# Feed-forward layers of an encoder on one core: four low parts made by ScalarE and adding transfers in place of VectorE, and one bank's copy put ahead of a high part

## The chip, the cores and the metric

The kernel runs on one core of one Trainium2 chip. The metric is the device time of one execution in microseconds, as a median of several runs. The profile that is read here is of one execution and has its own time.

## What is computed

The program is the trunk of a bidirectional encoder: two interleaved layers (attention, then a gated short convolution as token mixer), each followed by a squared-ReLU feed-forward layer and a gated embedding. The two request groups have 512 and 256 tokens and share the weights; the kernel runs them as 768 columns. The change is in the feed-forward part, the line with `mlp_w_up`:

```python
for i in range(DEPTH):                      # 2 layers
    h = rms_norm(x, norm_mix[i])
    x = x + (window_attention if i % 2 == 0 else short_conv)(h, ...)
    h = rms_norm(x, norm_mlp[i])
    x = x + jnp.square(jax.nn.relu(h @ mlp_w_up[i])) @ mlp_w_down[i]   # 1024 -> 4096 -> 1024
    gate = jax.nn.sigmoid(rms_norm(x, norm_ple[i]) @ ple_w_gate[i])
    x = x + (p[i] @ ple_w_proj[i]) * gate
return rms_norm(x, final_norm)
```

All of it is float32. The kernel splits each operand of a matmul into a high part in the matmul's own rounded type (fp32r) and a low part, the remainder, and adds three products: high by high, high by low, low by high.

## The kernel before

**The seven products.** In the feed-forward layers a product of two by two blocks is done with seven products instead of eight (Strassen's scheme), so weights and activations are also needed in sums. For the weights of one job (`Weights7`, two fetched tiles of 128x1024, `wraw`) these are: `direct` (keys w11, w12), `w22`, `s32` (the sum of which s3 and s2 are the halves) and `s14` (s1, s4). `sums32` and `sums14` form the sums on VectorE (L479, L480, L484, L485) in the tiles `sum0` and `sum1`. Each group then needs a high part (a copy on ScalarE, L504, into `whi`, `zhi` or `vhi`) and a low part (`wlo`, `zlo`, `vlo`). `s32` goes to the `z` tiles, of which there is one pair; `w22` to the `v` tiles, also one pair.

**Two ways to make a low part.** `low` (L532 for weights, L424 for activations) is one VectorE subtraction: source minus high part. `added` and `sum_added` do it without VectorE: ScalarE writes the negated high part into the low tile (L515, L524, L429), and then a DMA issued by GpSimd (POOL in the profile) adds the source onto it as it lands (L517 from DRAM for `w22`, L525 from the tile `sum0`, L430 from an activation tile). Before the change `w22` is done the second way in all these jobs, `s32` only once in a layer (in the last up job).

**Jobs.** A layer has 16 up jobs (each 256 of the 4096 hidden columns) and 16 down jobs, each of seven products. A product is 12 matmuls of 128x384. The order is written out by hand, `up` and `down` name the instructions of ScalarE, VectorE and TensorE in the order in which these engines run them, and each job prepares the weights of the next (`v = make()`). After the first two ups come seven groups of four jobs: an up, two downs, an up. So each group runs as first down, second down, **odd up**, and then the **even up** of the next group; the even up follows directly on an odd up and stands directly before a **first down**. Ups run their products in the order w11, s3, s2, w12, s1, w22, s4, into the banks a, b, a, c, a, d, a; so do downs, with two banks for each letter. Before s2 may write into bank a, ScalarE must have copied a to c (L1370; in downs L1454): that is "the first bank's copy". After s3 ScalarE copies b to p (L1377), after s2 it copies a to d (L1382).

**Activations of an up.** An up job leaves two tiles y1, y2. Their squares, four sums (t1, t3 in y1's tile; t4, t2 in y2's: L408 to L414) and their high and low parts are made by a list of eight steps (`acts_of`), which the next up works off between its own instructions (`late`): square y1; high part of x11; high part of x21 and x22 with their low parts and t1, t3; t4 and t2; high part of t1 and t3 (L418); high part of t4 and t2; low part of t1 and t3 (L424); low part of t4 and t2 (L424). The odd up works off the list of the even up before it, the even up that of the odd up before it, in both cases for the down jobs that come next; the first down begins right after the even up has worked off its list, and its product s2 reads, in its first four matmuls, the high and low part of t2 of one up and then of the other.

**What GpSimd does.** In these layers POOL issues only the adding transfers, in program order. SP issues the fetches of `wraw` (L111), of which three tiles exist.

## Time and profile before

| | |
|---|---|
| median of 3 runs | 1596.95 us (1595.84 to 1600.51) |
| the profiled execution | 1596.31 us, of which its span is 1594.5 us |
| mean granted TensorE clock | 0.995 |
| one group of four jobs (28 products) | 56.18 us, seven times a layer |
| TensorE idle (span less busy) | 48.5 us |
| VectorE and ScalarE busy from 490 to 900 us | 372.5 and 253.9 of 410 us |
| adding transfers issued by POOL | 72 (62 of L517, 6 of the gate weights L1643, 2 each of L430 and L525) |

The page gives, for each engine, its busy time; "PE" is TensorE's matmuls and "PEld" its weight loads. The recorded duration of a matmul (326 ns) is its way through the array; the next begins about 163 ns after it, so twelve take 1.95 us. In the timeline a row is a run of equal instructions with its start and length in us; in brackets stands how long the engine had been idle, and what ended that.

### The profile page before, as it was taken

The page shows a single profiled execution, that of the slowest core. Times are in us where ns is not written, and L with a number is a line of the kernel's source. Part 1 is how long each engine was busy: PE and PEld are TensorE (multiplying, and loading weights), DVE is VectorE, ACT ScalarE, POOL GpSimd, SP SyncE. Part 2 cuts the span into 40 slices and gives each one's busy share as a digit, 9 for nine tenths or more (in the row PEclk, how much of TensorE's full clock was granted, in tenths as well). Part 3 has the DMA queues.
Part 4 walks back from the last instruction along what each step waited for, and adds up shares of the span by engine and source line. Part 5 has one row for each costly group of instructions (what it writes and reads, how often), then busy time and mean ns, then how long its engine had stood idle before and what let it go on. Part 6 is the DMA issues. An engine that isn't in the chain of part 4 may idle for free.

```text
span 1594.5 us, 24379 instructions
## 1 busy us (share of the span) xinstructions
PE 1546.0 (97%) x9375; PEld 1485.2 (93%) x9375; DVE 1404.2 (88%) x2300; ACT 977.4 (61%) x1566; POOL 82.5 (5%) x116
## 2 busy tenths in 40 slices
PE   9999999999999999999989999999999999999996
PEld 7988889999999999999989999999999999999985
DVE  8599898899999899999898887869999999999997
ACT  7478766866566556657764344556656656655764
POOL 0211000010000000001000000000000000000000
PEclk9999999999999999999999999999999999999998
DMA  8854413443333333335512212122333333333432
GB/s 278 214 138 131 138 45 99 120 108 82 96 100 100 100 94 78 94 100 143 154 60 80 79 67 84 63 78 68 99 100 99 96 90 81 98 100 99 113 102 103
DMA packets 57461, 166.35 MB, mean 104 GB/s; under 512 B 7249, under 2 KB 10833, under 8 KB 57345
## 3 DMA queue, kind: packets, MB, share of 16 engines
q1 hardware_dynamic: 45440, 139.89, 27.2%
q0 software_dynamic: 11904, 24.91, 8.9%
q8 instruction: 73, 1.20, 0.3%
q14 instruction: 44, 0.35, 0.1%
HBM read 143.02 MB, written 10.48 MB: 96 GB/s over the span
## 4 chain that ended last, share of the span: by engine, by line
PE 46%; DVE 38%; ACT 10%; issue 4%; DMA 1%; SPq 0%; DVEq 0%; ACTq 0%
PE a L180 17%; PE mm L180 8%; PE B L180 4%; DVE t L424 4%; PE b L180 4%; PE C L180 4%; DVE wlo L532 4%; DVE y L1146 3%; DVE zlo L532 3%; PE gate L180 2%; DVE act L463 2%; PE c L180 2%; ACT y L1149 1%; DVE sum L480 1%; DVE sum L479 1%
## 5 line engine op out<-in xcount | busy, mean ns | idle before, releaser
L180 PE MATMUL a<-xs,whi 128*128 128x384 f32 x624 | 115.6, 328 | 3.0 <-DVE y L1393 1.6
L180 PE MATMUL a<-t,zhi 128*128 128x384 f32 x568 | 111.2, 329 | 2.9 <-ACT c L1370 2.9
L180 PE MATMUL a<-t,whi 128*128 128x384 f32 x568 | 109.4, 326 | 0.0
L180 PEld LDWEIGHTS a<-xs,whi 128*128 128x128 f32 x624 | 102.5, 189 | 5.8 <-DVE low L2047 2.5
L180 PE MATMUL b<-t,zhi 128*128 128x384 f32 x552 | 106.8, 326 | 0.3 <-DVE t L424 0.3
L504 ACT ACTIVATE vhi<-wraw 128x512 fp32r<-128x512 f32 x71 | 44.6, 628 | 98.9 <-PE B L180 81.3
L180 PE MATMUL a<-act,whi 128*128 128x384 f32 x512 | 104.1, 326 | 0.0
L1459 DVE TENSOR_TENSOR x<-x,a 128x384 f32<-128x384 f32 x128 | 70.3, 555 | 37.2 <-PE a L180 37.2
L180 PEld LDWEIGHTS a<-t,zhi 128*128 128x128 f32 x568 | 93.7, 189 | 7.7 <-ACT c L1370 6.4
L532 DVE TENSOR_TENSOR wlo<-wraw,whi 128x1024 fp32r<-128x1024 f32 x74 | 90.3, 1220 | 10.9 <-ACT whi L504 10.9
L1149 ACT ACTIVATE y<-y 128x768 f32<-128x768 f32 x62 | 51.9, 837 | 71.6 <-DVE y L1146 71.5
L180 PEld LDWEIGHTS a<-t,whi 128*128 128x128 f32 x568 | 94.9, 189 | 0.6 <-ACT d L1561 0.6
L532 DVE TENSOR_TENSOR wlo<-sum,whi 128x1024 fp32r<-128x1024 f32 x71 | 86.8, 1222 | 8.8 <-ACT whi L504 8.8
L180 PEld LDWEIGHTS b<-t,zhi 128*128 128x128 f32 x552 | 92.3, 189 | 0.9 <-DVE t L424 0.9
L504 ACT ACTIVATE whi<-sum 128x1024 fp32r<-128x1024 f32 x71 | 74.5, 1049 | 21.2 <-PE a L180 18.4
L180 PEld LDWEIGHTS a<-act,whi 128*128 128x128 f32 x512 | 86.6, 189 | 0.0
L504 ACT ACTIVATE zhi<-sum 128x1024 fp32r<-128x1024 f32 x71 | 74.9, 1054 | 19.1 <-DVE sum L480 19.1
L418 ACT ACTIVATE t<-y 128x768 fp32r<-128x768 f32 x64 | 53.8, 840 | 51.9 <-DVE y L409 45.5
L532 DVE TENSOR_TENSOR zlo<-sum,zhi 128x1024 fp32r<-128x1024 f32 x69 | 84.0, 1218 | 0.0
L504 ACT ACTIVATE whi<-wraw 128x1024 fp32r<-128x1024 f32 x76 | 79.7, 1048 | 3.7
L180 PE MATMUL mm<-xs_mix,whi 128*128 128x512 f32 (+1 forms) x320 | 77.3, 331 | 0.2 <-DVE pjs L610 0.2
L180 PE MATMUL b<-t,zlo 128*128 128x384 f32 x276 | 63.1, 332 | 10.7 <-DVE zlo L532 10.7
(335 smaller groups left out, 4389.6 us busy)
## 6 DMA issues: line engine op xcount, KB each, us to landing
wraw<-in_up SPq DMA_DIRECT2D x64, 512.0 KB, 4.2
wraw<-in_down SPq DMA_DIRECT2D x64, 512.0 KB, 4.4
wraw<-in_w_in SPq DMA_DIRECT2D x24, 512.0 KB, 3.4
vlo<-in_down POOLq DMA_DIRECT2D x32, 256.0 KB, 6.0
wraw<-in_gate SPq DMA_DIRECT2D x16, 512.0 KB, 3.8
vlo<-in_up POOLq DMA_DIRECT2D x28, 256.0 KB, 5.8
pj<-pjs SPq DMA_DIRECT2D x16, 384.0 KB, 2.9
wraw<-in_w_q SPq DMA_DIRECT2D x8, 512.0 KB, 4.7
```

Source lines behind the costliest of these rows:

```text
L180: pe.matmul(ps, lhsT=w, rhs=rhs, **flags)
L418: act.activation(t[0][:], (self.q1, self.q2)[i][:], AF.Copy)
L424: dve.tensor_tensor(lo[:], (self.q1, self.q2)[i][:], hi[:].bitcast(F32), ALU.subtract)
L463: dve.tensor_tensor(lo[:], self.q2[:], hi[:].bitcast(F32), ALU.subtract)
L479: dve.tensor_tensor(a[:, :512], r1[:, :512], r2[:, :512], ALU.add)
L480: dve.tensor_tensor(a[:, 512:], a[:, :512], r2[:, 512:], ALU.add)
L504: act.activation(hi[:], src, AF.Copy)
L532: dve.tensor_tensor(lo[:], src, hi[:].bitcast(F32), ALU.subtract)
L1146: dve.scalar_tensor_tensor(t[:, o:e], src, 0.0, r[:, o:e], op, ALU.mult)
L1149: act.activation(t[:], t[:], AF.Square)
L1459: dve.tensor_tensor(t[:, o : o + H], t[:, o : o + H], f, op)
```

## The change

It has four parts. In `acts_of` the last step, the low part of t4 and t2, is `added(1)` in place of `low(1)`: a negated copy on ScalarE and an adding transfer of 384 KB. In `up`, in `down` and in the first of the last two downs (`down_first`) the high part of `s32` is followed at once by `sum_added`'s negated copy and an adding transfer of 512 KB, and the subtraction on VectorE (`w.low("s32")` in the next job) finds nothing left to do. In `up` one step of the list that stood between product w11 and the first bank's copy now stands behind the copy. And `rest` in `down_first` loses its `low("s32")`.

```diff
@@ acts_of
                 lambda: e.high(0),
                 lambda: e.high(1),
                 lambda: e.low(0),
-                lambda: e.low(1),
+                lambda: e.added(1),
@@ up
             product7(a, w, "w11", xs, True)
-            if not first:
-                late()
             c = bank("A" if first else "C", "c")[:, :H]
             act.activation(c, a, AF.Copy)
-            late(5 if first else 1)
+            late(5 if first else 2)
@@ up
             if seven:
                 v.sums14()
-                (v.sum_added if final else lambda: v.high("s32"))()
+                v.sum_added()
@@ down, and the same line in down_first
             v.sums14()
-            v.high("s32")
+            v.sum_added()
@@ down_first
             def rest():
                 added(top, H, a, ALU.add)
-                v.low("s32")
                 v.low("s14")
                 less(p)
```

The two functions that it now calls more often stand as they were:

```python
def added(self, i):                       # Sums, activations
    hi, lo = self.t[i]
    act.activation(lo[:], hi[:].bitcast(F32), AF.Copy, scale=-1.0)
    nc.gpsimd.dma_start(lo[:], (self.q1, self.q2)[i][:], accum_op=ALU.add)

def sum_added(self):                      # Weights7
    self.high("s32")
    self.due.remove("s32")
    hi, lo, src = self.parts["s32"]
    act.activation(lo[:], hi[:].bitcast(F32), AF.Copy, scale=-1.0)
    nc.gpsimd.dma_start(lo[:], src, accum_op=ALU.add)
```

ScalarE's queue in an even up of the first layer, before (y and t are the activation tiles, t_5339 and t_5342 the high parts of t1, t3 and of t4, t2):

```order
L504 ACTIVATE whi<-sum 128x1024
L1149 ACTIVATE y_5232<-y_5232 128x768
L450 ACTIVATE act<-y_5232 128x384
L1370 ACTIVATE c<-a 128x384
L454 ACTIVATE act<-y_5233 128x768
L1377 ACTIVATE p<-b 128x384
L1382 ACTIVATE d<-a 128x384
L418 ACTIVATE t_5339<-y_5232 128x768
L418 ACTIVATE t_5342<-y_5233 128x768
L504 ACTIVATE zhi<-sum 128x1024
L504 ACTIVATE whi<-wraw 128x1024
L504 ACTIVATE vhi<-wraw 128x512
```

The same stretch of ScalarE's queue in the changed kernel, from the first bank's copy on:

```order
L1368 ACTIVATE c<-a 128x384
L450 ACTIVATE act<-y_5246 128x384
L454 ACTIVATE act<-y_5247 128x768
L1375 ACTIVATE p<-b 128x384
L1380 ACTIVATE d<-a 128x384
L418 ACTIVATE t_5352<-y_5246 128x768
L418 ACTIVATE t_5355<-y_5247 128x768
L504 ACTIVATE zhi<-sum 128x1024
L524 ACTIVATE zlo<-zhi 128x1024
L504 ACTIVATE whi<-wraw 128x1024
L429 ACTIVATE t_5356<-t_5355 128x768
L504 ACTIVATE vhi<-wraw 128x512
```

The copy of a to c has moved ahead of the high part of x11 (L450), and two negated copies, L524 and L429, stand around the high part of `direct`.

POOL's queue before, over two groups of four jobs, is these rows (each is the transfer of `w22`, one for a job):

```order
L517 DMA vlo<-in_down 128x512 x2
L517 DMA vlo<-in_up 128x512 x2
L517 DMA vlo<-in_down 128x512 x2
L517 DMA vlo<-in_up 128x512 x2
L517 DMA vlo<-in_down 128x512 x2
```

POOL's queue in the changed kernel, from an odd up over the even up and the two downs to the next odd up (t_5207 and t_5356 are the low parts of t4, t2):

```order
L525 DMA zlo<-sum 128x1024
L430 DMA t_5207<-y_4822 128x768
L517 DMA vlo<-in_up 128x512
L525 DMA zlo<-sum 128x1024
L430 DMA t_5356<-y_5247 128x768
L517 DMA vlo<-in_down 128x512
L525 DMA zlo<-sum 128x1024
L517 DMA vlo<-in_down 128x512
L525 DMA zlo<-sum 128x1024
L517 DMA vlo<-in_up 128x512
```

A group of four jobs had four transfers in POOL's queue and has ten; in an up job they are three, in the order zlo, t, vlo. In the whole program VectorE's queue loses 86 instructions (56 of L532 into zlo, 30 of L424), and ScalarE and POOL gain 86 each.

## The prediction
> **What bounds the kernel now.** First the page's busy times, then TensorE's waits:

> ```profile
> PE 1546.0 (97%) x9375; PEld 1485.2 (93%) x9375; DVE 1404.2 (88%) x2300; ACT 977.4 (61%) x1566; POOL 82.5 (5%) x116
> ...
> PE b L180 <- DVE zlo L532: 10.7, 17, 0.7
> PE c L180 <- ACT xs L372: 4.6, 1, 4.6
> PE a L180 <- ACT c L1370: 2.9, 12, 0.2
> ```

> TensorE sets the end; what VectorE saves is worth only TensorE's waits. Two kinds recur in the feed-forward layers, and the change aims at both: on `zlo`, and on the first bank's copy c. The waits show too little, since a matmul's row (326 ns) covers half of a gap. The chain of waits in order of time gives a group's true cost:

> ```profile
> 459.74 1.98 PE a L180 x12
> 461.72 1.95 PE C L180 x12
> ...
> 515.92 1.98 PE a L180 x12
> ```

> A group takes 515.92 - 459.74 = 56.18 us; its 28 products of 1.95 us are 54.6. So **1.58 us are lost in a group**, 22 us in the 14. The timeline of an even up and the first down behind it shows where:

> ```profile
> 499.90 0.81 PE L180 MATMUL b<-t,zlo 128*128 128x384 f32 x4
> 500.00 0.52 ACT L450 ACTIVATE act<-y 128x384 fp32r<-128x384 f32 x1
> 500.43 0.47 ACT L1370 ACTIVATE c<-a 128x384 f32<-128x384 f32 x1
> 500.96 1.57 PE L180 MATMUL a<-t,zhi 128*128 128x384 f32 x8 [0.24 <-ACT c L1370]
> ...
> 512.83 0.81 PE L180 MATMUL b<-t,zhi 128*128 128x384 f32 x4
> 513.08 1.22 DVE L532 TENSOR_TENSOR zlo<-sum,zhi 128x1024 fp32r<-128x1024 f32 x1
> 514.35 0.59 PE L180 MATMUL b<-t,zlo 128*128 128x384 f32 x2 [0.71 <-DVE zlo L532]
> ```

> Four matmuls after 499.90 (0.65 us), s2 could begin at 500.55; it begins at 500.96 with its next matmul 0.1 late too: 0.5 lost. Four after 512.83 `zlo` is wanted at 513.48 and comes at 514.35: 1.0 lost.

> **The change, part by part.** Prices of one instruction:

> ```profile
> L532 DVE TENSOR_TENSOR zlo<-sum,zhi x69: 1214/1218/1225, 325.3 to 1498.9; 128x1024 fp32r<-128x1024 f32 x69
> L424 DVE TENSOR_TENSOR t<-y,t 128x768 fp32r<-128x768 f32 x64 | 60.8, 952 | 0.1
> L524 ACT ACTIVATE zlo<-zhi x2: 1057/1057/1057, 716.8 to 1477.3; 128x1024 fp32r<-128x1024 f32 x2
> L429 ACT ACTIVATE t<-t x2: 824/832/839, 317.7 to 321.0; 128x768 fp32r<-128x768 f32 x2
> ```

> VectorE loses 56 x 1.22 + 30 x 0.95 = 97 us, ScalarE gains 56 x 1.06 + 30 x 0.83 = 84 us. Neither is a term of the sum: ScalarE, at 61%, has room on average. What counts is when POOL's transfers land, and here a second set of rows decides:

> ```profile
> 319.48 0.88 POOL L430 DMA_DIRECT2D t<-q  x1 [5.75 <-ACT t L418]
> 321.00 0.84 ACT L429 ACTIVATE t<-t 128x768 fp32r<-128x768 f32 x1
> 323.62 0.89 POOL L430 DMA_DIRECT2D t<-q  x1 [3.26 <-ACT whi L504]
> 325.54 0.64 ACT L515 ACTIVATE vlo<-vhi 128x512 fp32r<-128x512 f32 x1
> 327.75 0.88 POOL L517 DMA_DIRECT2D vlo<-in_up  x1 [3.24 <-ACT t L418]
> ...
> 718.27 0.87 POOL L525 DMA_DIRECT2D zlo<-sum  x1 [10.02 <-ACT zlo L524]
> 721.22 0.63 ACT L515 ACTIVATE vlo<-vhi 128x512 fp32r<-128x512 f32 x1
> 723.27 0.90 POOL L517 DMA_DIRECT2D vlo<-in_down  x1 [4.12 <-issue]
> ...
> t<-q POOLq DMA_DIRECT2D x2, 384.0 KB, 3.8
> zlo<-sum POOLq DMA_DIRECT2D x2, 512.0 KB, 4.7
> ```

> Read each transfer against the ScalarE copy that it needs. The copy for the transfer of 323.62 ended at 321.84, that for 327.75 at 326.18, that for 723.27 at 721.85: POOL sat 1.4 to 1.8 us with its input ready. What had just happened is the landing of the transfer before: 319.48 + 3.8 = 323.3, 323.62 + 3.8 = 327.4, 718.27 + 4.7 = 723.0. Each time POOL went on 0.3 us later. **POOL has one of these whole-tile transfers under way at a time**: a zlo holds it for 4.7 + 0.3 = 5.0 us, a t for 4.1. Before the change that costs nothing, for its transfers come 13 us apart:

> ```profile
> 490.98 1.06 ACT L504 ACTIVATE zhi<-sum 128x1024 fp32r<-128x1024 f32 x1 [0.16 <-DVE sum L480]
> 494.73 1.22 DVE L532 TENSOR_TENSOR wlo<-wraw,whi 128x1024 fp32r<-128x1024 f32 x1
> 494.97 0.63 ACT L515 ACTIVATE vlo<-vhi 128x512 fp32r<-128x512 f32 x1
> 496.01 0.88 POOL L517 DMA_DIRECT2D vlo<-in_up  x1 [12.49 <-ACT vlo L515]
> ...
> 506.26 1.06 ACT L504 ACTIVATE zhi<-sum 128x1024 fp32r<-128x1024 f32 x1 [0.48 <-DVE sum L480]
> 508.21 0.81 PE L180 MATMUL d<-t,vlo 128*128 128x384 f32 x4
> ...
> DMA to landing us min/median/max: 4.0/5.9/8.1
> ```

> The last row is line 517's. Free POOL starts 0.41 after the copy (494.97 + 0.63 to 496.01). Now the walk, on these rows' clock, through the three transfers of the odd up and the three of the even up:

> - Odd up: `zhi` ends at 492.04, its negated copy at 493.1, zlo is issued at 493.5 and lands at 498.2, before 499.90, where it is read. t goes at 498.5 and lands at 502.3, vlo goes at 502.6. For vlo I take 5.0 to land (between 4.0 and 5.9, since the fetches that it shares the engines with have passed by then): 507.6. The even up wants it at 507.8 (508.21 less the 0.4 that the copy saves, next): on time, at the median 0.7 late.
> - The copy c in the even up: ScalarE's queue is later there, since `high("direct")` of the odd up now stands behind two negated copies and ends at 492.04 + 1.06 + 0.83 + 1.05 less some overlap, near 494.85; VectorE's wlo waits for it (494.73 before) and y2 stands behind wlo. That makes 0.15 later than before, while one high part (0.43 from start to start at 500.00) no longer stands ahead of c. It ends at 500.90 + 0.15 - 0.43 = 500.62, and s2 wants it at 500.55: **0.1 lost** in place of 0.5.
> - Even up: the copy p has to wait for t (502.3; that transfer reads the buffer that p takes), which has slack: before s1 nothing waits for what stands behind p. VectorE's path to `zhi` (x21's high part, four sums, `sums32`) is as long as before and starts 0.15 later: 506.4. With both copies ScalarE is at 508.5, zlo is issued at 508.95 and lands at 513.65. The first down, 0.4 earlier, wants it at 513.05: **0.6 lost** in place of 1.0.
> - t of the even up: its negated copy ends near 510.2, POOL is free only at 513.95; t lands at 517.75. The first down, begun at 510.45 (512.83 less w11's 1.95 and the 0.4), reads it in the fourth matmul of s2: 510.45 + 2 x 1.95 + 0.6 + 3 x 0.163 = 515.45. **2.3 lost**, where nothing was lost before.
> - vlo of the even up goes at 518.05 and lands at 523.05; w22 wants it at 517.75 + 9 x 0.163 + 2 x 1.95 + 0.65 = 523.8: hidden.
> - In both downs only zlo and vlo are in the queue, 10.3 us of 13.7; hidden. A down's zlo, issued some 10 us into the job, lands 15 in and is wanted 16.3 in.

> The sum is 0.1 + 0.6 + 2.3 = 3.0 us in a group at the landings recorded. Those of zlo and t are of two quiet transfers each; with one fetch or two beside them I add 0.1 to each of the three that lead to t, so **3.3 us** against 1.58: 14 x 1.7 = 24 us (the first group of a layer begins otherwise, and is counted like the rest). Against the profiled execution's 1596.31 that is 1620, and 1621 on the scale of the median, 1596.95. Bounds from both sides: 3.0 and nothing more gives 14 x 1.4 = 20; 0.5 more for each landing adds 2.3 (five landings in a row, less a little slack), so 14 x 3.7 = 52 and 1649. `rest` in `down_first` saves 1.2 us of VectorE's time twice, at most 2 us in all.

> [...]

> **Rivals.**
> 1. *POOL doesn't wait* (faster, or the same). For it speak small transfers:

> ```profile
> 102.38 4.58 POOL L776 DMA_DIRECT2D bias<-skew  x8 [42.08 <-DVE mx L814]
> bias<-skew POOLq DMA_DIRECT2D x32, 96.0 KB, 4.3
> ```

> Eight go out in 4.6 us though each takes 4.3 to land. If whole tiles do so in the changed kernel, t of the even up is issued at 510.6, lands at 514.4 and is no longer waited for; c's 0.1 and zlo's 0.6 stay. That is 0.9 less a group, 12 us faster: 1585. If the overlapping transfers slow each other by 1 us, zlo costs what VectorE's did, and it is the same. It decides at a t landing before 515.45. Against it stand all three pairs above. [...]
> 2. *Crowding.* With ten transfers for four a group, landings go up by 1 us each, still inside line 517's spread of 4.0 to 8.1. Then the loss is 3.0 + 4.7 = 7.7 a group, 14 x 6.1 = 86: 1682.
> 3. *The clock.* After TensorE's one wait of 4.6 us the clock was halved; after one of 2.3 it was not:

> ```profile
> 824.00:831.00 7.00, 4.18 (x12) 3.68 (x13) 5.87 (x8) 4.72 (x5) 0.00 (x0) 0.52 0.01 2
> 1555.00:1566.00 11.00, 8.43 (x71) 7.88 (x70) 6.67 (x12) 5.87 (x9) 0.00 (x0) 1.00 0.08 24
> PE ss L180 <- ACT ah L105: 2.3, 1, 2.3
> ```

> My 2.3 us lie on the safe side; at 1 to 2 us more each group could pay another 3.5 us (7 us at half speed), up to 49 in all: 1670.

> **How the numbers follow.** POOL one at a time, with the landings above up to 0.5 us more: 0.78. Rivals 2 and 3, slower still: 0.08. Rival 1: 0.14, of which 0.08 faster and 0.06 the same. The forecast is 1621 us. Its own range is 1615 to 1653; to hold 8 in 10 I widen it below to 1606, for an overlap in part. A measurement tells 0.3%, about 5 us, from no change; so faster 0.08, the same 0.06, slower 0.86.

> **What would show it.** POOL's rows in an even up: zlo, t, vlo each 0.3 us behind the landing before (right), or less than 2 us apart (wrong). TensorE's waits: `zlo <- DVE` gone, and in its place a wait on the DMA of t at the fourth matmul of the first down's s2, about 2 us, 14 times; c's wait gone or nearly. A group near 58 us. VectorE near 1307 us busy. Wrong would be the forecast if t's wait is missing, or if the same wait stands on vlo in the even up, which would mean slower landings.

## The result, and the profile after

The changed kernel takes 1647.95 us (1645.57 to 1650.31, 4 runs) where before takes 1598.06 us beside it (1595.84 to 1600.51, 4 runs): a ratio of 1.0313, 95% interval 1.0296 to 1.033. It is 50 us slower; 24 were forecast. The profiled execution has a span of 1648.5 us against 1594.5.

First the page's busy times and DMA queues, then TensorE's waits (engine, operands and line; who was waited for; us in total, times, longest):

```profile
PE 1567.1 (95%) x9375; PEld 1502.1 (91%) x9375; DVE 1330.8 (81%) x2214; ACT 1050.2 (64%) x1652; POOL 158.7 (10%) x202
...
q1 hardware_dynamic: 45440, 139.89, 24.9%
q0 software_dynamic: 24288, 66.07, 22.5%
...
zlo<-sum POOLq DMA_DIRECT2D x58, 512.0 KB, 4.8
...
t<-y POOLq DMA_DIRECT2D x30, 384.0 KB, 4.4
```

```profile
PE a L180 <- DMA t<-y: 36.9, 14, 3.6
PE B L180 <- DMA zlo<-sum: 4.6, 2, 2.5
...
PE a L180 <- DVE y L1391: 3.7, 9, 1.7
...
PE a L180 <- ACT d L1380: 1.8, 3, 0.8
PE d L180 <- DMA vlo<-in_up: 1.7, 2, 0.8
```

`zlo <- DVE` and `c <- ACT` have gone from the top. In their place stands t, 14 times, 2.3 to 3.6 us of idle time each and 2.6 in the mean. Below it stand four small kinds for which the forecast counted no loss; one of them, on vlo in the even up, it had named as a sign of slower landings. A group took 59.9 us in the first layer and 59.1 in the second, where 58 were forecast. POOL's timeline, from an odd up to the first down two jobs later:

```profile
503.43 0.90 POOL L525 DMA_DIRECT2D zlo<-sum  x1 [9.16 <-ACT zlo L524]
508.60 0.88 POOL L430 DMA_DIRECT2D t<-y  x1 [4.27 <-ACT y L1149]
513.14 0.90 POOL L517 DMA_DIRECT2D vlo<-in_up  x1 [3.66 <-issue]
518.95 0.88 POOL L525 DMA_DIRECT2D zlo<-sum  x1 [4.90 <-DVE y L1391]
524.27 0.90 POOL L430 DMA_DIRECT2D t<-y  x1 [4.44 <-ACT whi L504]
```

The queue is as forecast: zlo, t, vlo, zlo, t, each of the last four 0.3 us behind the landing of the one before. (The names in brackets are the last events that the profile saw, and had nothing to do with it.) TensorE in the first down's s2, and the windows around it (us; then busy time and instructions of PE, PEld, DVE, ACT and POOL; granted clock; DMA share; GB/s):

```profile
525.41 0.65 PE L180 MATMUL a<-t,zhi 128*128 128x384 f32 x3
528.74 0.43 PE L180 MATMUL a<-t,zhi 128*128 128x384 f32 x1 [2.68 <-DMA t<-y]
529.00 0.49 PE L180 MATMUL a<-t,zlo 128*128 128x384 f32 x2
529.33 1.20 PE L180 MATMUL a<-t,zhi 128*128 128x384 f32 x4
```

```profile
525.90:528.70 2.80, 0.16 (x1) 0.00 (x0) 2.77 (x4) 0.20 (x1) 0.00 (x0) 1.00 0.79 164
528.70:533.00 4.30, 4.26 (x16) 4.27 (x17) 1.30 (x3) 2.18 (x4) 0.89 (x1) 0.61 0.41 61
```

The stall stands at the matmul that was named. Behind it four matmuls take 1.20 us instead of 0.81: the granted clock was 0.50, for 3.41 us (0.61 is the mean over the second window). The trace has eight such stretches in the two feed-forward layers, before has none.

To account for the time I add up, over the two feed-forward layers, by how much the start of each matmul lies more than 0.163 us behind the one before it, by what was late (us; half clock: matmuls that only run slower). The 0.163 is the distance from start to start in an unbroken run, and only this is used: no run shows what a matmul does in the rest of its row. The kernels are those of the next section:

| | t and c | zlo in a first down | half clock | zlo at a layer's end | all else | sum |
|---|---|---|---|---|---|---|
| before | 6.7 | 13.6 | 0 | 0 | 8.4 | 28.7 |
| after | 41.6 | 3.6 | 11.8 | 5.4 | 19.0 | 81.4 |
| no_reorder | 41.6 | 3.8 | 5.8 | 4.1 | 8.9 | 64.2 |
| end_undone | 41.4 | 4.3 | 9.4 | 0 | 18.4 | 73.4 |
| early_t | 0.2 | 0.2 | 0 | 0 | 8.1 | 8.5 |

After less before is 52.7 us, nearly the whole difference of the spans (54.0).

### The profile page after: what moved, and what is told of

It reads as the page before. It is cut to its first block, busy times and chain, and to the rows that moved or that the text cites. A ratio compares the mean times of both kernels' runs of the same rounds, so it can differ in the third digit from the quotient of the medians.

```text
span 1648.5 us, 24671 instructions
## 1 busy us (share of the span) xinstructions
PE 1567.1 (95%) x9375; PEld 1502.1 (91%) x9375; DVE 1330.8 (81%) x2214; ACT 1050.2 (64%) x1652; POOL 158.7 (10%) x202
## 4 chain that ended last, share of the span: by engine, by line
PE 43%; DVE 26%; ACT 14%; issue 9%; DMA 7%; POOL 1%; DVEq 0%; SPq 0%; ACTq 0%; POOLq 0%
PE a L180 17%; PE mm L180 8%; DMA t<-y 4%; PE C L180 4%; PE B L180 4%; PE b L180 2%; ACT whi L504 2%; DVE wlo L532 2%; PE c L180 2%; DVE act L463 2%; ACT y L1149 1%; DVE sum L480 1%; ACT act L454 1%; DVE sum L479 1%; PE pt L847 1%
## 5 line engine op out<-in xcount | busy, mean ns | idle before, releaser
L180 PE MATMUL a<-t,zhi 128*128 128x384 f32 x568 | 117.8, 338 | 36.9 <-DMA t<-y 36.9
L180 PEld LDWEIGHTS a<-t,zhi 128*128 128x128 f32 x568 | 96.3, 192 | 44.2 <-DMA t<-y 41.1
L532 DVE TENSOR_TENSOR wlo<-sum,whi 128x1024 fp32r<-128x1024 f32 x71 | 87.0, 1225 | 46.3 <-ACT whi L504 46.3
L180 PE MATMUL a<-xs,whi 128*128 128x384 f32 x624 | 115.5, 328 | 5.1 <-DVE y L1391 3.7
L180 PE MATMUL a<-t,whi 128*128 128x384 f32 x568 | 109.7, 327 | 1.8 <-ACT d L1380 1.8
L532 DVE TENSOR_TENSOR wlo<-wraw,whi 128x1024 fp32r<-128x1024 f32 x74 | 90.5, 1222 | 25.4 <-ACT whi L504 24.8
L180 PEld LDWEIGHTS a<-xs,whi 128*128 128x128 f32 x624 | 102.8, 189 | 8.9 <-DVE y L1391 6.4
L180 PE MATMUL b<-t,zhi 128*128 128x384 f32 x552 | 106.8, 327 | 0.3 <-DVE t L424 0.3
L180 PE MATMUL a<-act,whi 128*128 128x384 f32 x512 | 104.2, 326 | 0.0
L180 PEld LDWEIGHTS a<-t,whi 128*128 128x128 f32 x568 | 94.8, 189 | 3.3 <-ACT d L1380 2.7
L180 PEld LDWEIGHTS b<-t,zhi 128*128 128x128 f32 x552 | 92.4, 189 | 0.9 <-DVE t L424 0.9
L504 ACT ACTIVATE whi<-sum 128x1024 fp32r<-128x1024 f32 x71 | 74.5, 1049 | 21.3 <-PE a L180 18.4
L525 POOL DMA_DIRECT2D zlo<-sum x58 | 51.2, 883 | 372.6 <-PE a L180 142.1
L180 PEld LDWEIGHTS a<-act,whi 128*128 128x128 f32 x512 | 86.6, 189 | 0.0
L504 ACT ACTIVATE zhi<-sum 128x1024 fp32r<-128x1024 f32 x71 | 74.9, 1055 | 17.7 <-DVE sum L480 17.7
L504 ACT ACTIVATE vhi<-wraw 128x512 fp32r<-128x512 f32 x71 | 44.2, 623 | 60.1 <-PE B L180 60.1
L504 ACT ACTIVATE whi<-wraw 128x1024 fp32r<-128x1024 f32 x76 | 79.3, 1044 | 1.2 <-PE C L180 1.2
L418 ACT ACTIVATE t<-y 128x768 fp32r<-128x768 f32 x64 | 53.3, 838 | 38.9 <-DVE y L409 35.3
L180 PE MATMUL mm<-xs_mix,whi 128*128 128x512 f32 (+1 forms) x320 | 77.3, 331 | 0.2 <-DVE pjs L610 0.2
L1452 ACT ACTIVATE B<-a 128x384 f32<-128x384 f32 x60 | 28.5, 475 | 71.6 <-PE a L180 70.6
## 6 DMA issues: line engine op xcount, KB each, us to landing
wraw<-in_up SPq DMA_DIRECT2D x64, 512.0 KB, 4.5
wraw<-in_down SPq DMA_DIRECT2D x64, 512.0 KB, 4.5
zlo<-sum POOLq DMA_DIRECT2D x58, 512.0 KB, 4.8
wraw<-in_w_in SPq DMA_DIRECT2D x24, 512.0 KB, 3.4
t<-y POOLq DMA_DIRECT2D x30, 384.0 KB, 4.4
wraw<-in_gate SPq DMA_DIRECT2D x16, 512.0 KB, 4.6
```

The costliest lines, as they stand in the source:

```text
L180: pe.matmul(ps, lhsT=w, rhs=rhs, **flags)
L418: act.activation(t[0][:], (self.q1, self.q2)[i][:], AF.Copy)
L504: act.activation(hi[:], src, AF.Copy)
L525: nc.gpsimd.dma_start(lo[:], src, accum_op=ALU.add)
L532: dve.tensor_tensor(lo[:], src, hi[:].bitcast(F32), ALU.subtract)
L1452: act.activation(t, f, AF.Copy)
```

## Experiments

Each kernel is the changed one with the edit shown, unless it says otherwise. Times are medians, ratios are to before in the same comparison, with the 95% interval.

### What holds POOL back

**ring1024** and **before_ring** double the setting `dynamic_dma_scratch_size`, which the expectations call POOL's room or descriptor room, in the changed kernel and in before.

```diff
-BACC = dict(dynamic_dma_scratch_size=512)
+BACC = dict(dynamic_dma_scratch_size=1024)
```

> [...] Theory A, POOL waits for room: two whole-tile transfers fit, so in an up job t is issued within 1.5 us of zlo, the 14 waits of TensorE on t (36.9 us of idle) and the halved clocks behind them go, and the time is 1580 to 1592 us (12 or more below before). Rival B, POOL waits for the landing before, whatever the room: every issue still comes 0.3 us behind a landing, 1648 us. Rival C, the transfers are slow because ten of them crowd the DMA engines: issues come early, landings go up to 6 us or more, the wait on t stays at over 1.5 us, 1625 to 1645 us.

> The kernel of before with the doubled descriptor room of POOL, and nothing else: the control for ring1024 (1680). Theory A (ring1024 lost time because zlo, t, vlo and two fetches then stand in the DMA engines together): with one adding transfer per job nothing can overlap, so 1595 to 1600. Rival B (the room itself, or the place of the tiles behind it, costs time): 1605 or more.

ring1024: 1679.91 us, 1.0512 (1.0491 to 1.0534). before_ring: 1597.08 us, 0.9996 (0.9986 to 1.0005). POOL's timeline of ring1024 in an odd up, its landing of t, and one window (columns as above):

```profile
510.36 0.87 POOL L525 DMA_DIRECT2D zlo<-sum  x1 [10.02 <-ACT zlo L524]
511.09 1.04 POOL L430 DMA_DIRECT2D t<-y  x1
513.22 0.90 POOL L517 DMA_DIRECT2D vlo<-in_up  x1 [1.09 <-ACT vlo L515]
...
t<-y POOLq DMA_DIRECT2D x30, 384.0 KB, 8.6
...
515.00:519.00 4.00, 4.00 (x26) 3.91 (x25) 2.29 (x3) 3.64 (x7) 0.00 (x0) 1.00 1.00 272
```

The setting is what made POOL issue one at a time: doubled, it lets t go 0.7 us after zlo. But t now needs 8.6 us to land instead of 4.4, TensorE's waits on it grow from 36.9 to 54.8 us, and the kernel loses another 32 us: the time lies outside all three expected ranges. The setting alone costs before nothing. While t is on its way the DMA share is 1.00 (from 515 to 519 us). Three adding transfers and two fetches of 512 KB are under way then: from 510 to 522 us POOL's queue takes 57.9% of the time of the 16 engines and the fetches' queue 22.4%, and the two fetches take 6.7 and 8.4 us to land, where at the same place in the changed kernel they took 4.4 and 4.9. So the first rival's issue came about, and its landing did not. zlo and t, both in POOL's queue, land one behind the other, near 514.9 and 518.8 us (4.5 and 7.7 us after their issues). How the engines divide their time between the two queues was not shown.

### Which transfers cost

**no_t** takes t back to VectorE; **no_zlo** takes `s32` back to VectorE (except in the last up of a layer, as before) and leaves t and the copy's place; **zlo_downs** does that in the ups alone.

```diff
@@ no_t, acts_of
-                lambda: e.added(1),
+                lambda: e.low(1),
@@ no_zlo and zlo_downs, up
-                v.sum_added()
+                (v.sum_added if final else lambda: v.high("s32"))()
@@ no_zlo, down and down_first
-            v.sum_added()
+            v.high("s32")
@@ no_zlo, rest
+                v.low("s32")
```

> The changed kernel with the low part of t4, t2 by VectorE again (low(1) for added(1)); zlo stays with the transfers, and the copy c stays ahead. Theory A: an up job has two transfers, zlo and vlo, 9 to 10 us of POOL's time in 13.7; no wait on t; zlo costs up to 0.6 us in the first down and once at each layer's end 2.5 us: 1588 to 1602 us. Rival D, the negated copies make ScalarE late and that costs the time: zlo's two copies stand where they stood, so most of the loss stays, 1625 us or more.

> The changed kernel with s32's low part by VectorE again everywhere but in each layer's last up (as before); t stays with the transfer, c stays ahead. Theory A: an up job has t and vlo in POOL's queue, t is issued when its copy is ready and lands 4.4 us later, about 1 us before it is read; VectorE has lost 28 us: TensorE's waits of a group (1.58 us) nearly all go, 1574 to 1584 us, faster than before by 1% or more. Rival C, crowding or late copies: t is still waited for, over 1 us in each of 14 groups, 1600 us or more.

> The changed kernel with the low part of s32 by VectorE in the ups (except the last of a layer) and by transfer in the downs. Theory A (the whole loss comes from zlo, t and vlo standing one behind the other in an up; in the downs the zlo transfer is hidden): as no_zlo, 1591, plus the wait at a layer's end that the zlo of the last downs brings (5 us in all): 1592 to 1598. Rival B (the downs' transfers also slow the ups': they take the DMA engines from the fetches, which then come late): 1600 to 1625. Rival C (VectorE's relief in the downs is worth something): below 1590.

no_t: 1601.22 us, 1.0024 (1.0014 to 1.0033). no_zlo: 1591.33 us, 0.9959 (0.9944 to 0.9974). zlo_downs: 1596.04 us, 0.999 (0.9981 to 0.9998). Either half of the change alone is within half a per cent of before; only both together cost 50 us. no_t lies in the range of its theory A; no_zlo lies between its two ranges, since with t alone (no_zlo) t is still waited for:

```profile
PE a L180 <- DMA t<-y: 9.6, 14, 1.2
```

That is 0.7 us each. zlo_downs lands where its theory A put it, 5 us behind no_zlo: the downs' transfers are hidden, except the one at the layer's end.

**t_first** keeps all transfers and puts t ahead of zlo in every up.

```diff
@@ t_first, up
             late(2)
             if seven:
                 v.sums14()
+                late(2)
                 v.sum_added()
-            late()
+            else:
+                late()
```

> The changed kernel with t's negated copy and transfer ahead of those of zlo in every up; the same transfers, in the order t, zlo, vlo. Theory A (three transfers one behind the other, whichever goes last in line is late): t's wait goes, and zlo lands 4.4 + 0.3 + 4.8 us behind the landing of the odd up's vlo, near 528.4 on the changed kernel's clock, where the first down's s3 wants it at 524.0: a stall of about 4 us on zlo in each group, the clock halved behind it, 1665 to 1690. Rival B (t's late step was the fault, as early_t suggests for the kernel without zlo): 1600 to 1635.

1765.38 us, 1.1042 (1.1019 to 1.1065): far beyond both ranges. First its waits, then POOL's and SP's timelines in an odd up, and its landing of zlo:

```profile
PE b L180 <- DMA zlo<-sum: 122.2, 28, 6.6
...
523.30 0.90 POOL L430 DMA_DIRECT2D t<-y  x1 [7.70 <-DVE t L424]
527.50 0.88 POOL L525 DMA_DIRECT2D zlo<-sum  x1 [3.30 <-PE a L180]
535.62 0.90 POOL L517 DMA_DIRECT2D vlo<-in_up  x1 [7.24 <-issue]
...
526.44 1.07 SPq L111 DMA_DIRECT2D wraw<-in_down  x2
...
zlo<-sum POOLq DMA_DIRECT2D x58, 512.0 KB, 6.9
```

The wait has moved to zlo, as theory A said, but zlo comes late from both ups of a group (28 waits), and each is longer: two fetches now go out just ahead of it, and it lands 7.8 us after its issue (535.62 less 0.3, less 527.50). Over the whole trace the 58 zlo took 6.9 us in the median; in the changed kernel, where none of the 58 went out with a fetch of `wraw` under way, they took 4.8. The expectation had only the even up and a landing of 4.8. So the order in the line did not help, and the zlo that started just behind two fetches took more than half as long again. Two fetches further ahead came with a smaller delay: in the changed kernel t starts 3.4 and 2.6 us behind two fetches (508.60 against 505.25 and 505.99) and takes 4.4 in the median, against 3.8 for the two quiet ones of before.

### The terms that the forecast had at nothing

**hold_clock** gives TensorE 12 matmuls to do in the stall; **end_undone** takes the zlo transfer out of the first of the last two downs.

```diff
@@ hold_clock, s2 of a first down, first bank, ahead of its fourth matmul (spare[0] is bank b, copied to p by then)
+                                for n in range(12):
+                                    matmul(spare[0], hi[:, c0], ph[0][0], start=n == 0, stop=n == 11, skip_group_check=True)
@@ end_undone, down_first
-            v.sum_added()
+            v.high("s32")
@@ end_undone, rest
+                v.low("s32")
```

> The changed kernel with 12 more matmuls in each first down, put between the third and the fourth matmul of s2 (where t is waited for). They write a bank whose result has been copied out and is overwritten later, so the output is the same; they give TensorE 1.95 us of work in a stall of 2.5 to 3.8 us. Theory A (the clock is halved because TensorE stood idle for 2.5 us or more; this is the term that the forecast put at nothing): the idle time before the fourth matmul falls to 0.5 to 1.8 us, the half-clock events of the feed-forward layers go from 8 to 2 or fewer, the t stalls end when they ended before, and the time falls by 8 to 12 us, to 1636 to 1640. Rival B (the clock is halved for another reason, or the events cost nothing since what follows is waited for anyway): 1646 to 1650. Rival C (the added matmuls delay s2 itself or slow the transfer): over 1652.

> The changed kernel with the low part of s32 in the first of the last two downs by VectorE again (one zlo a layer, two in all). Theory A (TensorE's wait on zlo at the end of a layer, 2.40 and 2.97 us, is this transfer's landing, and stood in no term of the forecast): this wait goes, nothing comes in its place, and the time falls by 4 to 6 us to 1642 to 1644. Rival B (VectorE, which then has this subtraction in the last down, makes the wait as long): 1647 to 1649.

hold_clock: 1637.64 us, 1.0255 (1.0241 to 1.027). TensorE at the same place:

```profile
522.49 0.76 PE L180 MATMUL a<-t,zhi 128*128 128x384 f32 x3
523.27 2.22 PE L180 MATMUL b<-t,zhi 128*128 128x384 f32 x12
525.63 0.43 PE L180 MATMUL a<-t,zhi 128*128 128x384 f32 x1
525.89 0.49 PE L180 MATMUL a<-t,zlo 128*128 128x384 f32 x2
526.22 0.81 PE L180 MATMUL a<-t,zhi 128*128 128x384 f32 x4
```

From the first of the three matmuls to the fourth it takes about as long as before (525.63 - 522.49 = 3.14 us, where the changed kernel has 528.74 - 525.41 = 3.33), but behind it four matmuls take 0.81 us. Of eight halved stretches one is left, and the kernel is 10 us faster with 27 us more work for TensorE. That is theory A, but for one number: the idle time left ahead of the fourth matmul is 0.1 to 1.3 us, not 0.5 to 1.8. So it was the idle time that halved the clock: with it filled, the mean granted clock is 0.995 where the changed kernel has 0.986. end_undone: 1641.93 us, 1.0275 (1.0262 to 1.0288), 6 us faster; the wait on zlo at the layer's end is gone and nothing came in its place. This is that transfer in the changed kernel, with the two fetches at its side:

```profile
759.68 0.88 POOL L525 DMA_DIRECT2D zlo<-sum  x1 [6.91 <-PE B L180]
768.43 0.90 POOL L517 DMA_DIRECT2D vlo<-in_down  x1 [7.87 <-issue]
...
759.82 0.89 SPq L111 DMA_DIRECT2D wraw<-in_gate  x2
```

It is read 6.2 us after its issue, and at the median landing of 4.8 nothing would be waited for. But two fetches for the next part of the layer go out 0.1 and 0.7 us behind it, and it takes 8.4 us to land (8.8 in the second layer).

### The first bank's copy

**reorder_only** is before with the copy moved and nothing else; **no_reorder** is the changed kernel with the copy where it was, **odd_old** and **even_old** put it back in one kind of up.

```diff
@@ no_reorder, up (odd_old: the same where u is odd, even_old: where u is even)
+            if not first:
+                late()
             c = bank("A" if first else "C", "c")[:, :H]
             act.activation(c, a, AF.Copy)
-            late(5 if first else 2)
+            late(5 if first else 1)
```

> Before with only the copy c moved ahead of the high part in the up jobs; no new transfer. By the walk: 12 waits on c of 0.5 us become 0.1, the wait on zlo (1.0) stays: 1591 to 1594 us. Rival: what comes later in ScalarE's queue delays VectorE's zlo by as much, 1597 to 1599 us.

> The changed kernel with the first bank's copy where it stood before. Theory A (the walk gave 0.4 us a group for it, which t's wait behind it does not hide since t's transfer waits on ScalarE's queue of the same up): 1648 to 1656. Rival B (what c loses, the wait on t at the end of the same job takes back, as t lands by POOL's queue and not by TensorE's progress): 1645 to 1649.

> The changed kernel with the first bank's copy put back in the odd ups alone. Theory A (the move costs its 14 us there: the odd up follows a down, its copy must wait for product w11 to end, and the step that now stands behind it, the high parts of x21 and x22 and all of VectorE's sums after them, comes 0.8 us later and with it zlo, t and vlo of that up and t of the next): 1628 to 1636, as no_reorder or better. Rival B (the cost is in the even up): 1645 to 1652.

> The changed kernel with the first bank's copy put back in the even ups alone. Theory A (as for odd_old): no gain from it, 1646 to 1654. Rival B (the cost is in the even up): 1632 to 1638.

reorder_only: 1596.95 us, 0.9992 (0.9983 to 1.0001), no difference, so the gain that the walk gave the move is missing. no_reorder: 1633.79 us, 1.0224 (1.0209 to 1.024): **14 us faster** than the changed kernel, outside both expectations. odd_old: 1636.03 us, 1.0237 (1.0222 to 1.0252). even_old: 1649.76 us, 1.0317 (1.03 to 1.0334). The cost is in the odd ups. Here is ScalarE there, first in before, then in the changed kernel, then in no_reorder, from the high part of s14 to that of s32:

```profile
482.88 1.06 ACT L504 ACTIVATE whi<-sum 128x1024 fp32r<-128x1024 f32 x1 [0.66 <-PE a L180]
483.84 0.51 ACT L450 ACTIVATE act<-y 128x384 fp32r<-128x384 f32 x1
484.26 0.83 ACT L454 ACTIVATE act<-y 128x768 fp32r<-128x768 f32 x1
485.15 0.47 ACT L1370 ACTIVATE c<-a 128x384 f32<-128x384 f32 x1
```

```profile
492.79 1.06 ACT L504 ACTIVATE whi<-sum 128x1024 fp32r<-128x1024 f32 x1 [0.66 <-PE a L180]
493.75 0.51 ACT L450 ACTIVATE act<-y 128x384 fp32r<-128x384 f32 x1
495.06 0.47 ACT L1368 ACTIVATE c<-a 128x384 f32<-128x384 f32 x1 [0.81 <-PE a L180]
495.45 0.83 ACT L454 ACTIVATE act<-y 128x768 fp32r<-128x768 f32 x1
...
500.88 1.06 ACT L504 ACTIVATE zhi<-sum 128x1024 fp32r<-128x1024 f32 x1 [0.16 <-DVE sum L480]
```

```profile
491.22 1.06 ACT L504 ACTIVATE whi<-sum 128x1024 fp32r<-128x1024 f32 x1 [0.66 <-PE a L180]
...
498.52 1.05 ACT L504 ACTIVATE zhi<-sum 128x1024 fp32r<-128x1024 f32 x1
```

In an odd up ScalarE is early, since a down stands before it. The copy c must wait for product w11, and in before the step L454 (the high parts of x21 and x22) filled that time. Behind the copy it starts 2.66 us after L504 instead of 1.38, with VectorE's sums of the activations and the sums of s32 behind it. So `zhi` starts 8.09 us after L504 in the changed kernel, 8.10 in before, and 7.30 without the move: relieved of its subtractions, VectorE would have brought `zhi`, and the whole line of five transfers behind it, 0.8 us forward; the move took that back.

The time is not lost at t, whose column in the table is the same in both kernels. It is lost in the even up that follows, where by the table's measure the waits on y, d and vlo come to 11.7 us in the changed kernel and to 3.3 in no_reorder, and in the clock (11.8 and 5.8). Three rows of TensorE's waits, of reorder_only, even_old and odd_old:

```profile
PE a L180 <- DVE y L1391: 3.7, 13, 1.7
...
PE a L180 <- ACT c L1371: 4.2, 12, 0.4
...
PE a L180 <- DVE y L1394: 2.1, 2, 1.6
```

In reorder_only the wait on c is gone and one on y stands in its place, which before has once. With the move in the odd ups TensorE waits in the even up for y (reorder_only, the changed kernel) or, where the copy is back in the even ups, for c (even_old). Only odd_old, with the move in the even ups alone, is nearly rid of both.

### The sum, and a faster version

**three_out** takes the three terms out together: hold_clock, end_undone and no_reorder in one kernel.

> The changed kernel with the three terms taken out that the forecast had at nothing or the wrong way: the copy where it was (14 us by no_reorder), no zlo transfer in the first of the last downs (6 us by end_undone), 12 matmuls in the stall on t so that the clock holds (10 us by hold_clock, but 6 us of half clock are left in no_reorder). Theory A (what then remains is the forecast's own sum, 24 us, and the 5.6 us that it credited to the copy): the terms add up, 1633.8 - 6 - 6 = 1622, between 1617 and 1627. Rival B (the terms overlap, since each shifts the others' waits onto t): 1629 or more.

1621.72 us, 1.0152 (1.0136 to 1.0168), within 0.3 us of theory A. The terms add up, when the halved clock that no_reorder also takes away is counted once.

**early_t** starts from no_zlo and does t's negated copy and its transfer one step earlier; **early_t_old_c** is that with the copy where it was in before.

```diff
@@ early_t, up of no_zlo
                 (v.sum_added if final else lambda: v.high("s32"))()
-            late()
+            late(2)
             product7(c, w, "w12", xs, False)
```

> As the kernel that leaves s32 to VectorE (no_zlo, 1591), but the negated copy and the transfer of t stand one step earlier in an up: behind the high part of s32 and ahead of the high part of direct, which puts its issue 1.0 us earlier and ahead of two fetches. Theory A (t's 0.7 us at the fourth matmul of s2 is what remains of the landing): this wait goes in nearly all of the 14 groups, about 0.7 us each, less what the high part of direct loses: 1581 to 1586. Rival B (t's landing depends on the fetches beside it more than on its issue): the wait stays, 1590 to 1593. Rival C (the high part of direct, 0.8 us later, makes wlo and the next product w11 late): 1594 or more.

> early_t (1577) with the first bank's copy where it stood before, behind the step of the list. Theory A (with the other waits gone, c's wait of 0.5 us a group is worth its full 6.7 us, where reorder_only by itself gained 1 us): 1581 to 1585. Rival B (the copy's place makes no difference here either): 1576 to 1579.

early_t: 1577.06 us, 0.9872 (0.9859 to 0.9885); early_t_old_c: 1577.09 us, 0.9868 (0.9853 to 0.9883). **Both beat before by 1.3%**, and with it every other kernel here. early_t lies below all its ranges, 4 us under theory A's. The first row is of no_zlo, the next two are of early_t: POOL's transfer of t in an even up, and what follows it in early_t; the last row is early_t's busy times:

```profile
507.85 0.90 POOL L430 DMA_DIRECT2D t<-y  x1 [10.02 <-ACT t L429]
...
503.81 0.90 POOL L430 DMA_DIRECT2D t<-y  x1 [9.06 <-ACT t L429]
508.94 0.88 POOL L517 DMA_DIRECT2D vlo<-in_down  x1 [4.23 <-ACT y L1149]
...
PE 1540.5 (98%) x9375; PEld 1489.1 (94%) x9375; DVE 1380.7 (88%) x2270; ACT 996.6 (63%) x1596; POOL 109.1 (7%) x146
```

Two fetches go out 0.1 and 1.0 us behind t in no_zlo, and 1.1 and 1.9 us behind it in early_t; t takes 6.9 us to land there and 4.8 here (508.94 less 0.3, less 503.81). So the earlier step gave more than its 1 us. No wait on t is left, nor on zlo (VectorE has time for it once t's subtraction is gone), nor on c. By the table's measure no_zlo loses 21.8 us and early_t 8.5, and nothing in these 8.5 recurs from group to group. Here the copy's place makes no difference: theory A of early_t_old_c fell.

## Why the direction was right and the size wrong

Three steps of the forecast failed: the halved clock, taken as out of reach; the zlo at a layer's end, taken as hidden; and the moved copy, booked as a gain where it was a loss. The mechanism that it rested on, the line of transfers that ends in a wait on t, was right, and the size of that term was nearly so.

**Right.** POOL one at a time (each row 0.3 us behind a landing); the wait on t at the fourth matmul of the first down's s2, 14 times; zlo's wait on VectorE gone; the downs hidden (zlo_downs). The walk through the transfers holds in detail. Counted from L504 in the odd up, it had the first zlo issued at 493.5 - 482.88 = 10.62 us; the trace has 503.43 - 492.79 = 10.64. The t at the end of the line it had landing 34.87 us after L504; TensorE went on with it at 528.74 - 492.79 = 35.95. The vlo that it had on time in the even up came 1.0 us late in this group, since its transfer took 5.5 us (518.95 less 0.3, less 513.14) and not 5.0.

**The sum** had 46.2 us of loss in 14 groups where before had 22.1. The terms, against the table:

- *t and c, 14 x (2.3 + 0.1) and the allowance of 14 x 0.3:* 37.8 us forecast, 41.6 measured. From row to row the transfers of the line took 5.17, 4.54, 5.81, 5.32 and, to TensorE's start, 4.47 us; the walk had 5.0, 4.1, 6.35 (with a wait for ScalarE), 5.0 and 3.8, 24.25 in all against 25.31. The two quiet transfers of before were too short a price for t, 3.8 us against a median of 4.4. The upper bound of the range had 0.5 us for each landing and takes this in. *zlo in the first down* came out lower, 3.6 for 8.4.
- *The clock, rival 3.* "My 2.3 us lie on the safe side" failed. It took one wait of 2.3 us without a halved clock as a limit. The 14 stalls were 2.3 to 3.6 us long, and halved stretches followed in 6 of the groups and at both layers' ends: 11.8 us by the table, 10 us by hold_clock. Their length alone does not decide: one of 2.33 us (it ends at 1139.32) was followed by a halved stretch, one of 2.57 (at 1377.43) was not. Rival 3 had 0.08 together with rival 2, and in part it came true.
- *The layer's end* was in no step: that the downs are hidden was worked out for a down in the middle of a layer, with a landing of about 5 us. The zlo of the first of the last two downs has two fetches right behind it and takes 8.4 and 8.8. 5.4 us by the table, 6 by end_undone (both halved stretches at the layers' ends go with it).
- *The copy c* was booked as a gain of 0.4 us a group. It cost 14 us, and this is the largest of the three errors. The walk took `zhi` in the odd up at its old distance from L504, 8.10 us, and that is what it got; what was missed is that without the move it would have been 0.8 us less. I had followed the moved step in the even up only, where ScalarE is late, and not in the odd up, where it is early. In the table no_reorder differs by 10 us in "all else" (waits on y, d, C and vlo) and by 6 us of half clock. How 0.8 us in an odd up becomes each of these waits was not followed step by step.

Clock, layer's end and copy taken out together leave 1621.7 us, 24 us above before: the forecast's number, for a kernel without the three terms that it had left out or had the wrong way. That the two numbers are alike to a us is luck: without its credit of 0.4 us a group for the copy the forecast for that kernel would have been 30 us, and the longer landings and the smaller zlo term offset each other in part.

**Rival 1** (POOL doesn't wait) was wrong for this kernel, and ring1024 shows that it would not have helped: its premise that t, issued at once, lands after its own 3.8 us did not hold there (8.6 us in the median, with a DMA share of 1.00 from 515 to 519 us). **Rival 2** (crowding) did not come about at a queue that goes one at a time (landings of 4.4 and 4.8 for 3.8 and 4.7), but it did in ring1024, in t_first and at the layers' ends.

VectorE's busy time on the page fell by 73 us, not by the 97 worked out. No term rested on it, and the work did go: the rows of the two subtractions fell from 84.0 to 15.8 us and from 60.8 to 32.4, which is 97 together. The page counts time in which rows of VectorE overlap only once, and these overlaps fell from 136 to 113 us.

## What to carry to other kernels

Work moved off a busy engine onto a queue is priced by where the last transfer in line lands against its first reader, and by which fetches go out just before and behind it; two kinds of transfer that each cost nothing alone cost 50 us together here. A step that is moved has to be followed in every job that runs it: the place that was late in one kind of job filled idle time in the other. And a new stall of the length met here (2.3 to 3.6 us) is checked for what the clock does behind it, even where one wait of its length did no harm.
